# The latents' normalisation factors spread, and the latents scaled, ahead of the last projection panel

## The chip, the core and the metric

One core of a Trainium2 chip runs the whole program. The metric is the device time of one execution in microseconds (us); less is better. Five engines have instruction streams of their own: TensorE (PE, matmuls), VectorE (DVE), ScalarE (ACT), GpSimd (POOL) and SyncE (SP, which here only issues DMAs).

## What is computed

Two layers of a diffusion backbone over 512 latent tokens and 256 context tokens of width 1024. Layer 0 has 8 heads of multi-head latent attention (MLA) and 8 heads of neighbourhood attention side by side, then SwiGLU; layer 1 has sliding-window attention, then SwiGLU. What matters here is how the MLA heads get their inputs:

```
p = modulate(h) @ w_in                       # one input projection for all of layer 0
q_lat = rms_norm(p[..., :256], q_norm)       # query latent: 2 panels of 128 features
c_kv  = rms_norm(p[..., 256:384], kv_norm)   # key/value latent: 1 panel
k_rope = p[..., 384:416]
q = q_lat @ w_q_up ;  keys and values from c_kv
...
def rms_norm(x, gain):  return x * rsqrt(mean(x * x) + EPS) * gain
```

The neighbourhood heads take q, k, v from the other 1536 columns of the same projection.

## The kernel before

Features lie on the 128 partitions and the 768 tokens along a row (512 latents, `LATS`, then 256 context tokens, `CTXS`). A float32 product is made of three matmuls of operands split in a high and a low half (`split`: a cast on ACT, L340, and a difference on DVE, L341).

**Projections** (`projections`). One panel is 128 output features: `project` loads its weights, splits them and issues 24 matmuls of 512 columns for the latents (8 steps over the 16 high and low tiles of the modulated input, three each), then 24 of 256 columns for the context, each half in one PSUM bank, which ACT then evicts (L718). Banks come in a fixed rotation of tags by `PG` ("stsdtsd"); tag `d` has two buffers, `s` three, `t` two, `o` one. First come the panels of head pairs 0 and 1, then what the string `AFTER` says: 0, 1, 2 are the three latent panels (`lat_raw`), k the rope part, 5 to 8 the panels of q and k of pairs 2 and 3 (kept raw in `raws`), and r is `latent_roots`: squares of the three latents on ACT, sums over features on PE, square root on ACT, and the reciprocal on DVE (L973), which leaves one factor for each token in a column tile `sm`, six columns for each of two groups (the key/value latent, and the two query latents). Meanwhile DVE works on the modulation vectors (L234: products with an accumulated sum, two for each of two vectors), which `bg` deals out.

**Neighbourhood pairs** (`na_jobs`). For each of four head pairs, jobs make scores (L725, L726), take them into SBUF with bias and running minimum on DVE (L535, from `pss` banks; with `zeros` for context queries, with the bias tiles `nb` and `b` for the others), exponentials on ACT (L531, summing), transpose the result 128 x 128 on PE (L479), copy it (L470 on DVE, L471 on ACT) and multiply by the values (L525). `ORDER` says which other work is stepped beside which pair: `split_pair(2)` beside the first; `latent_norms` (n) and `split_pair(3)` beside the second; `mla_prepare` (m) beside the third. `split_pair` casts raw q on ACT (L1015), takes its low half on DVE (L1017), the same for k (L1023, L1024), and copies halves between partitions by DMAs on SP's queue. The bias tiles of the next pair come over that queue too.

**The step that is edited.** `latent_norms` runs `gained`. For each group, `gain` spreads the factors: a PE transposition of a column, broadcast to 128 x 128, for each block of 128 tokens (L346, four for the latents and two for the context, in a bank of tag `d` from `PQ`), which gives every partition the row of factors. DVE then scales each tile in place by gain and factor (L949), reading that bank. Then `gained` splits the scaled tiles.

**What sets the order.** The program is recorded as it is written; a scheduler then orders each engine's stream, by its own estimate of times and by priorities (work beside a pair has a lower one, `LOWER`), and each engine runs its stream in that order. Tiles of one tag share a ring of buffers: a tile waits until its buffer's last reader is done. The buffers of tag `b` that the pair splits and bias tiles take are those of the modulated input, which the last panel is the last to read.

Of the kernel before, what the change touches and what calls it, by code (L numbers as in the profile page):

```python
# [52 lines left out]
OUTQ = 1  # L53
E1, EF = 1, 1
ORDER = ("2", "n3", "m", "")
AFTER = "012k5r678"
PACE = (3, 3, 3, 3, 5, 5, 5, 6, 5, 5, 3, 2)
KC = (1, 1, 0)
VP = 0
# [39 lines left out]
def hybrid_kernel(ctx: ExitStack, tc, I, out):  # L99
# [6 lines left out]
    def T(tag, shape, dt=F32):  # L106
        count[0] += 1
        if tag not in SIZES:
            return sb.tile(shape, dt, tag=tag, name=f"{tag}_{count[0]}", bufs=BUFS.get(tag, 1))
        n = int(np.prod(shape[1:]))  # L110
        t = sb.tile([P, SIZES[tag] // (2 if dt == mybir.dt.bfloat16 else 4)], dt, tag=tag, name=f"{tag}_{count[0]}",
                    bufs=BUFS[tag])[: shape[0], :n]
        if len(shape) == 3:
            t = t.rearrange("p (a b) -> p a b", a=shape[1])
        return t

    def B(dt=F32, tag="b"):
        return T(tag, [P, NT], dt)
# [7 lines left out]
    def PG():  # L126

        ring[0] += 1
        return PS("stsdtsd"[ring[0] % 7])

    V, S, G, PE = nc.vector, nc.scalar, nc.gpsimd, nc.tensor
# [4 lines left out]
    def f(ap):  # L136
        return ap.bitcast(F32) if ap.dtype == F32R else ap
# [186 lines left out]
    def PQ():  # L324
        return PS("d")
# [10 lines left out]
    def split(src, eng=None, dst=None):  # L336

        p, n = src.shape
        h, lo = dst or (B(F32R), B(F32R))
        marks["cast"] = S.copy(h[:p, :n], src)  # L340
        marks["split"] = (eng or V).tensor_tensor(lo[:p, :n], src, f(h[:p, :n]), op=ALU.subtract)  # L341
        return h, lo

    def spread(o, col):

        return PE.transpose(o, col, ident)  # L346
# [337 lines left out]
    def put_q(ts, scale, hi=None, lo=None, after=()):  # L684


        def use(src, c):
            for side, t in enumerate(ts):
                r, x = slice(64 * side, 64 * side + 64), slice(64 - 64 * side, 128 - 64 * side)
                if scale is None:  # L690
                    behind((hi or S.copy)(t[r, c], src[r]), *after)
                    (lo or G.tensor_tensor)(t[x, c], src[r], f(t[r, c]), op=ALU.subtract)
                    continue
                S.activation(t[r, c], src[r], AF.Copy, scale=scale)
                V.scalar_tensor_tensor(t[x, c], src[r], scale, f(t[r, c]), op0=ALU.mult, op1=ALU.subtract)

        return use

    def put_k(ks, copies=True, hi=None):


        def use(src, c):
            for side, (k1, k2) in enumerate(ks):
                r, x = slice(64 * side, 64 * side + 64), slice(64 - 64 * side, 128 - 64 * side)
                (hi or S.copy)(k1[r, c], src[r])
                V.tensor_tensor(k2[r, c], src[r], f(k1[r, c]), op=ALU.subtract)
                if copies:
                    dma(k1[x, c], k1[r, c], G if dense[0] else None)
                    dma(k2[x, c], k2[r, c], G if dense[0] else None)
                else:  # L710
                    S.copy(k1[x, c], src[r])
                    V.tensor_tensor(k2[x, c], src[r], f(k1[r, c]), op=ALU.subtract)

        return use

    def put(t, rows=P, scale=1.0):
        def use(src, c):
            marks["put"] = S.activation(t[:rows, c], src, AF.Copy, scale=scale)  # L718

        return use  # L720
# [18 lines left out]
    def project(src, use, cols=(LATS, CTXS), m=P, every=2, eng=None, w=None, get=PQ):  # L739

        w = w or load_w(src, KT, m, eng)
        for c in cols:
            o, _ = banks([c], get, m)[0]
            for k in range(KT):
                mm3([(o, c)], (w[0][:, k : k + 1], w[1][:, k : k + 1]), A[k : k + 1], k == 0, k == KT - 1)
                if k % every == every - 1:
                    yield
            use(o, c)
# [26 lines left out]
    def first_norm(acc, c):  # L775
        n, d = (c.stop - c.start) // P, PM()
        col = T("sm", [P, 6, 2]).rearrange("p a b -> p (a b)")[:, :n]
        ins = [PE.matmul(d[:, i : i + 1], acc[:, i * P : (i + 1) * P], ones[:, :1], start=True, stop=True) for i in range(n)]
        run(ins[0], ins[-1])
        root = S.activation(col, d[:, :n], AF.Sqrt, bias=eps, scale=1.0 / D)  # L780
        V.reciprocal(col, col)
        return root, col
# [76 lines left out]
    _, diag = first_norm(acc, LATS)  # L859
# [8 lines left out]
    for c in range(4):  # L868
# [16 lines left out]
        if c == 3:  # L885
            _, diag = first_norm(acc, CTXS)
# [45 lines left out]
    def put_rope(t, tabs, swap, rows=P, scale=1.0, tag="b", eng=None):  # L932
        def use(src, c):
            if c is LATS:
                rope(t[:rows, c], src, tabs, swap, scale, tag, eng)
            else:
                S.activation(t[:rows, c], src, AF.Copy, scale=scale)

        return use

    def gain(tiles, g0, col):

        for c in (LATS, CTXS):
            d, n = PQ(), c.stop - c.start
            for i in range(n // P):
                at = c.start // P + i
                spread(d[:, i * P : (i + 1) * P], col[:, at : at + 1].to_broadcast([P, P]))
            for j, t in enumerate(tiles):
                V.scalar_tensor_tensor(t[:, c], t[:, c], gains[:, g0 + j : g0 + j + 1], d[:, :n], op0=ALU.mult, op1=ALU.mult)  # L949
        return tiles  # L950

    roots = []

    def latent_roots():

        d, m = PG(), NT // P
        groups = (lat_raw[2:], lat_raw[:2])
        col = T("sm", [P, 6, 2]).rearrange("p a b -> p (a b)")[:, : m * len(groups)]
        for i, tiles in enumerate(groups):
            acc = None  # L960
            for t in tiles:
                s = B(tag="p")
                S.activation(s, t, AF.Square)
                if acc is not None:
                    G.tensor_tensor(s, s, acc, op=ALU.add)
                acc = s
            for j in range(m):
                PE.matmul(d[:, i * m + j : i * m + j + 1], acc[:, j * P : (j + 1) * P], ones[:, :1], start=True, stop=True)
        for i, tiles in enumerate(groups):
            c = slice(i * m, i * m + m)  # L970
            S.activation(col[:, c], d[:, c], AF.Sqrt, bias=eps, scale=1.0 / (P * len(tiles)))
            roots.append(col[:, c])
        V.reciprocal(col, col)  # L973

    def gained(groups):

        for i, (tiles, g0) in enumerate(groups):
            res = [split(t, V) for t in gain(tiles, g0, roots[i])]
            groups[i] = res
            yield  # L980

# [3 lines left out]
    ON, lat_raw, kr = [], [None] * 3, []  # L985
# [3 lines left out]
    def projections():  # L989

        for p in range(2):
            yield from project(I["w_in0"][p], put_q(sets[p][0], 0.125), get=PG)
            yield from project(I["w_in0"][p + 4], put_k(sets[p][1], KC[0]), get=PG)
        for x in AFTER:
            if x in "012":
                lat_raw[int(x)] = B()
                yield from project(I["w_in0"][8 + int(x)], put(lat_raw[int(x)]), get=PG)
            elif x == "r":
                latent_roots()
            elif x == "k":  # L1000
                kr.append(B())
                yield from project(I["w_kr"], put_rope(kr[0], rope0, SWAP8, 32, tag="p"), m=32, get=PG)
            else:
                raws.append(B(tag="p"))
                i = int(x) - 5
                yield from project(I["w_in0"][(2, 6, 3, 7)[i]], put(raws[i], scale=(0.125, 1.0)[i % 2]), get=PG)
# [44 lines left out]
    def latent_norms():  # L1051
        groups = [(lat_raw[2:], 2), (lat_raw[:2], 0)]
        yield from gained(groups)
        wu["ckv"], wu["cq"] = groups
# [101 lines left out]
    for i, _ in enumerate(projections()):  # L1156
        n, r = PACE[i // 8], i % 8
        bg((r + 1) * n // 8 - r * n // 8)
# [45 lines left out]
    for k in range(KT):  # L1204
        t = B()
# [339 lines left out]
    for k in range(KT):  # L1545
        t = dr.tile([P, NL], F32, name=f"parked{k}")
# [78 lines left out]
    for k in range(KT):  # L1625
        t = B()
# [182 lines left out]
```

## Time and profile before

| | |
|---|---|
| median of 3 runs | 1558.43 us (1556.03 to 1559.27) |
| profiled execution | 1556.28 us, its span 1554.5 us |
| busy in the span | PE 97%, DVE 76%, ACT 49%, POOL 14% |
| granted TensorE clock | 0.996 |
| the six scalings L949 | 185.4 to 194.9 us |
| the reciprocal L973 | 156.3 us |

Busy time of PE goes by modelled ends, since matmuls are pipelined: a matmul's duration is longer than the distance to the next one's start. Times are counted from the start of the span. A row of the order of time has start, duration, engine, line, operation, written<-read and shape; in brackets stand the engine's idle time ahead of it and what ended it.

### The profile page before, as it was taken

How to read it: one execution, taken by the hardware profiler on the slowest of the kernel's cores; microseconds unless marked ns; L12 is line 12 of the kernel's file. 1: busy time of each engine (PE TensorE's matmuls, PEld its weight loads, DVE VectorE, ACT ScalarE, POOL GpSimd, SP SyncE). 2: the span in 40 equal slices, each digit the busy share in tenths (PEclk: the TensorE clock that was granted, in tenths of full speed). 3: DMA queues.
4: the chain of work that ended last, by engine and by line, in shares of the span. 5: the costliest groups of instructions: out<-in, count | busy, mean ns of one | idle time of the engine just before them, and what ended most of it. 6: DMA issues, size and time to landing. Idle time of an engine off the chain costs nothing.

```text
span 1554.5 us, 26373 instructions
## 1 busy us (share of the span) xinstructions
PE 1514.4 (97%) x9936; PEld 1364.3 (88%) x9936; DVE 1177.2 (76%) x2409; ACT 768.7 (49%) x1531; POOL 218.8 (14%) x272
## 2 busy tenths in 40 slices
PE   6999999999999999999999999999999999999998
PEld 4888887877999998999989998877889899899998
DVE  4799777686867686877768677779967779678685
ACT  4532587684555242433324335558746455454453
POOL 0021043110111102012021122650021000000001
PEclk9999999999999999999999999999999999999999
DMA  9674532023633636447365493200224223324222
GB/s 329 240 224 146 159 127 65 12 85 133 227 132 126 232 104 221 173 146 284 120 257 184 162 345 127 68 28 2 96 83 136 82 72 134 107 76 136 88 89 89
DMA packets 78736, 219.37 MB, mean 141 GB/s; under 512 B 10480, under 2 KB 17520, under 8 KB 78608
## 3 DMA queue, kind: packets, MB, share of 16 engines
q1 hardware_dynamic: 60848, 147.30, 28.4%
q0 software_dynamic: 16608, 68.81, 12.6%
q8 instruction: 78, 1.28, 0.3%
q10 hardware_dynamic: 1152, 1.57, 0.3%
q14 instruction: 50, 0.41, 0.1%
HBM read 186.97 MB, written 23.07 MB: 135 GB/s over the span
## 4 chain that ended last, share of the span: by engine, by line
PE 83%; DVE 8%; DMA 3%; ACT 3%; issue 2%; POOL 0%; SPq 0%; DVEq 0%; ACTq 0%; POOLq 0%
PE pss L1380 5%; PE pss L1379 5%; PE pss L1378 5%; PE pso L525 5%; PE psd L314 4%; PE pss L317 4%; PE pss L314 4%; PE psd L316 4%; PE pss L316 4%; PE psd L317 4%; PE pst L314 3%; PE pst L317 3%; PE pst L316 3%; PE pst L1380 3%; PE pst L1378 3%; PE pst L1379 3%
## 5 line engine op out<-in xcount | busy, mean ns | idle before, releaser
L303 ACT CAST wh<-wr 128x1024 fp32r<-128x1024 f32 (+2 forms) x148 | 115.5, 795 | 218.6 <-DMA wr<-in_w_dn_dram 44.2
L304 DVE TENSOR_TENSOR wl<-wr,wh 128x1024 fp32r<-128x1024 f32 (+2 forms) x145 | 130.7, 908 | 79.7 <-ACT wh L303 75.8
L531 ACT ACTIVATE p<-p,sm 128x512 f32<-128x512 f32 (+3 forms) x144 | 104.9, 730 | 28.4 <-DVE sm L535 28.0
L1378 PE MATMUL pss<-b,wh 128*128 128x384 f32 (+1 forms) x346 | 107.7, 312 | 0.6 <-ACT b L340 0.6
L1379 PE MATMUL pss<-b,wh 128*128 128x384 f32 (+1 forms) x346 | 107.9, 312 | 0.1
L1380 PE MATMUL pss<-b,wl 128*128 128x384 f32 (+1 forms) x346 | 107.2, 312 | 0.0
L270 DVE CUSTOM_DVE_ANT_0 p<-rope,cond 128x1024 bf16<-128x1024 f32 x64 | 76.8, 1219 | 15.4 <-DMA rope<-in_mod_w_dram 15.0
L316 PE MATMUL psd<-b,wh 128*128 128x512 f32 (+2 forms) x254 | 88.4, 348 | 0.1
L314 PE MATMUL psd<-b,wh 128*128 128x512 f32 (+2 forms) x214 | 78.7, 368 | 1.5 <-ACT b L444 0.6
L525 PE MATMUL pso<-ph,b 128*64 128x256 f32 (+1 forms) x384 | 78.1, 363 | 1.2 <-DVE ph L470 1.0
L525 PE MATMUL pso<-pl,b 128*64 128x256 f32 (+1 forms) x384 | 78.5, 363 | 0.0
L317 PE MATMUL psd<-b,wl 128*128 128x512 f32 (+2 forms) x214 | 77.0, 360 | 0.0
L260 POOL DMA_DIRECT2D rope<-in_mod_w_dram x48 | 25.6, 533 | 324.3 <-DVE mod L270 302.7
L1378 PE MATMUL pst<-b,wh 128*128 128x384 f32 (+1 forms) x226 | 70.6, 312 | 0.6 <-ACT p L1428 0.6
L1380 PE MATMUL pst<-b,wl 128*128 128x384 f32 (+1 forms) x226 | 70.6, 312 | 0.6 <-DVE wl L1366 0.6
L1365 ACT CAST wh<-pl 128x512 fp32r<-128x512 f32 x78 | 44.8, 619 | 52.2 <-PE pss L1379 22.8
L1379 PE MATMUL pst<-b,wh 128*128 128x384 f32 (+1 forms) x226 | 70.5, 312 | 0.0
L1365 ACT CAST wh<-wr 128x1024 fp32r<-128x1024 f32 x39 | 41.0, 1051 | 58.3 <-PE pst L1379 14.7
L316 PE MATMUL pss<-b,wh 128*128 128x256 f32 (+3 forms) x216 | 68.4, 317 | 0.0
L314 PE MATMUL pss<-st,wh 128*128 128x512 f32 (+2 forms) x198 | 67.1, 339 | 0.3 <-ACT wh L303 0.3
L317 PE MATMUL pss<-st,wl 128*128 128x512 f32 (+2 forms) x198 | 67.2, 339 | 0.1
L1378 PEld LDWEIGHTS pss<-b,wh 128*128 128x128 f32 x346 | 65.6, 190 | 1.1 <-ACT b L340 0.9
(603 smaller groups left out, 5275.3 us busy)
## 6 DMA issues: line engine op xcount, KB each, us to landing
wr<-in_w_gu_dram SPq DMA_DIRECT2D x88, 512.0 KB, 4.0
rope<-in_mod_w_dram POOLq DMA_DIRECT2D x48, 512.0 KB, 3.9
wr<-in_w_dn_dram SPq DMA_DIRECT2D x73, 256.0 KB, 2.9
wr<-in_w_out_dram SPq DMA_DIRECT2D x32, 512.0 KB, 4.3
p<-home POOLq DMA_DIRECT2D x40, 384.0 KB, 5.6
home<-p POOLq DMA_DIRECT2D x40, 384.0 KB, 5.3
wr<-in_w_in_dram SPq DMA_DIRECT2D x21, 512.0 KB, 4.2
ph<-in_mod_w_dram SPq DMA_DIRECT2D x24, 256.0 KB, 3.1
```

What stands on the lines that cost most here:

```text
L270: behind(V.tensor_tensor_reduce(out=T("p", [P, D], mybir.dt.bfloat16), in0=w, in1=cond[:, v, :], op0=ALU.mult, op1=ALU.add, scale=1.0, sca ...
L303: behind(S.copy(h, r), *after[:1])
L304: behind((G if eng else V).tensor_tensor(lo, r, f(h), op=ALU.subtract), *after[1:])
L314: ins = PE.matmul(o, wh[:, k], mh[:, c], start=first and k == 0, stop=False)
L316: PE.matmul(o, wh[:, k], ml[:, c], start=False, stop=False)
L317: PE.matmul(o, wl[:, k], mh[:, c], start=False, stop=last and k == n - 1)
L525: ins = PE.matmul(o[64 * i : 64 * i + 64, c], v(kt), t, start=n == 0, stop=n == len(moving[i]) - 1)
L531: S.activation(p[:, c], p[:, c], AF.Exp, bias=nm, scale=-1.0, accum_out=dn)
L1365: S.copy(h, t)
L1378: PE.matmul(o, wh, xh, start=first and k == 0, stop=False, skip_group_check=not first)
L1379: PE.matmul(o, wh, xl, start=False, stop=False, skip_group_check=not first)
L1380: PE.matmul(o, wl, xh, start=False, stop=k == 3, skip_group_check=not first)
```

## The change

`AFTER` gets a "g" between panel 7 and panel 8: there `gain` is called for both groups, so that the factors are spread and the latents scaled in the projections. `gained` keeps only the splits, which stay beside the second pair.

```diff
-AFTER = "012k5r678"
+AFTER = "012k5r67g8"
...
     def gained(groups):
 
-        for i, (tiles, g0) in enumerate(groups):
-            res = [split(t, V) for t in gain(tiles, g0, roots[i])]
+        for i, (tiles, _) in enumerate(groups):
+            res = [split(t, V) for t in tiles]
             groups[i] = res
             yield
...
             elif x == "r":
                 latent_roots()
+            elif x == "g":
+                for i, (tiles, g0) in enumerate(((lat_raw[2:], 2), (lat_raw[:2], 0))):
+                    gain(tiles, g0, roots[i])
```

Three lines are added ahead of L1003, so L1015, L1017, L1023 and L1024 of before are L1018, L1020, L1026 and L1027 of the change.

Where the instructions stand. PE at the end of the projections: before, the last matmul of the last panel (its context half, `pst`, behind its latents' half, `psd`) and then the first pair's scores.

```order
L316 MATMUL pst_1735<-b_113,wh_1696 128x256
L317 MATMUL pst_1735<-b_112,wl_1697 128x256
L725 MATMUL pss_1783<-st_654,st_652 128x256
L726 MATMUL pss_1783<-st_655,st_652 128x256
L725 MATMUL pss_1793<-st_656,st_653 128x256
L726 MATMUL pss_1793<-st_657,st_653 128x256
L725 MATMUL pss_1816<-st_654,st_652 128x256
L726 MATMUL pss_1816<-st_655,st_652 128x256
```

In the change the first group's six spreads stand ahead of that panel's context half; behind that half come (with the rest of the latents' half after the last row):

```order
L317 MATMUL pst_1757<-b_112,wl_1719 128x256
L725 MATMUL pss_1805<-st_654,st_652 128x256
L726 MATMUL pss_1805<-st_655,st_652 128x256
L725 MATMUL pss_1815<-st_656,st_653 128x256
L726 MATMUL pss_1815<-st_657,st_653 128x256
L725 MATMUL pss_1838<-st_654,st_652 128x256
L346 MATMUL psd_1703<-ident_r_86,sm_1504 128x128 x4
L346 MATMUL psd_1710<-ident_r_86,sm_1504 128x128 x2
L726 MATMUL pss_1838<-st_655,st_652 128x256
L725 MATMUL pss_1838<-st_654,st_652 128x256
L726 MATMUL pss_1838<-st_655,st_652 128x256
L314 MATMUL psd_1722<-b_98,wh_1718 128x512
```

The two halves of the panel have changed places, five of the scores come ahead of the second group's spreads, and the latents' half, whose bank is the one that `psd_1703` had, comes last.

ACT at the same place, before:

```order
L718 ACTIVATE p_1693<-psd_1700 128x512
L718 ACTIVATE p_1693<-pst_1735 128x256
L1015 CAST b_1803<-p_1415 128x768
L531 ACT_TABLE_LOAD
L531 ACTIVATE p_1784,sm_1773<-p_1784,sm_1774 128x256
```

and in the change:

```order
L718 ACTIVATE p_1715<-pst_1757 128x256
L1018 CAST b_1825<-p_1415 128x768
L1026 CAST b_1827<-p_1527 128x768
L718 ACTIVATE p_1715<-psd_1722 128x512
L531 ACT_TABLE_LOAD
```

The two casts of pair 2's split have moved ahead of the eviction of the latents' half; the table load and the first exponentials stand behind it.

DVE at the same place, before: the last products of the modulation (each followed by its sum, `128x1`) and the first takes.

```order
L234 ISA p_1729,mod_323_1409<-ph_1725,cond_66 128x512
L234 ISA mod_323_1409 128x1
L234 ISA p_1731,mod_323_1409<-pl_1727,cond_66,mod_323_1409 128x512
L234 ISA mod_323_1409 128x1
L238 SCALAR_TENSOR_TENSOR mod_323_1409<-mod_323_1409,modb_89 128x8
L234 ISA p_1760,mod_331_1435<-ph_1725,cond_66 128x512
L234 ISA mod_331_1435 128x1
L234 ISA p_1762,mod_331_1435<-pl_1727,cond_66,mod_331_1435 128x512
L234 ISA mod_331_1435 128x1
L238 SCALAR_TENSOR_TENSOR mod_331_1435<-mod_331_1435,modb_89 128x8
L535 ISA p_1784,sm_1774<-pss_1783,zeros_95 128x256
```

In the change, from the first scaling on:

```order
L949 SCALAR_TENSOR_TENSOR b_1220<-b_1220,mla_gain_690,psd_1693 128x512
L949 SCALAR_TENSOR_TENSOR b_1220<-b_1220,mla_gain_690,psd_1699 128x256
L234 ISA p_1753,mod_323_1409<-pl_1749,cond_66,mod_323_1409 128x512
L234 ISA mod_323_1409 128x1
L238 SCALAR_TENSOR_TENSOR mod_323_1409<-mod_323_1409,modb_89 128x8
L949 SCALAR_TENSOR_TENSOR b_1038<-b_1038,mla_gain_690,psd_1703 128x512
L949 SCALAR_TENSOR_TENSOR b_1132<-b_1132,mla_gain_690,psd_1703 128x512
L949 SCALAR_TENSOR_TENSOR b_1038<-b_1038,mla_gain_690,psd_1710 128x256
L949 SCALAR_TENSOR_TENSOR b_1132<-b_1132,mla_gain_690,psd_1710 128x256
L1020 TENSOR_TENSOR p_1415<-p_1415,b_1825 128x768
L234 ISA p_1782,mod_331_1435<-ph_1747,cond_66 128x512
L234 ISA mod_331_1435 128x1
```

The scalings stand among the last products, and the low halves of pair 2's split ahead of the last two products and thus of the first takes.

DVE in the second pair, from the first take with its bias tile, before:

```order
L535 ISA p_2065,sm_1950<-pss_2060,nb_1951 128x512
L535 ISA sm_1950 128x1
L535 ISA p_1960,sm_1950<-pss_1959,zeros_95 128x256
L535 ISA sm_1950 128x1
L1024 TENSOR_TENSOR st_2055<-p_1693,st_2054 128x768
L949 SCALAR_TENSOR_TENSOR b_1220<-b_1220,mla_gain_690,psd_2007 128x512
L470 COPY pl_1974<-pst_1969 128x512
L455 RECIPROCAL sm_2126<-sm_1773 128x12
L470 COPY pl_1998<-pst_1993 128x512
L535 ISA p_1984,sm_1950<-pss_1983,zeros_95 128x256
L535 ISA sm_1950 128x1
L535 ISA p_2089,sm_1950<-pss_2082,nb_1951 128x512
```

and in the change:

```order
L535 ISA p_2065,sm_1972<-pss_2060,nb_1973 128x512
L535 ISA sm_1972 128x1
L341 TENSOR_TENSOR b_2030<-b_1220,b_2029 128x768
L455 RECIPROCAL sm_2126<-sm_1795 128x12
L341 TENSOR_TENSOR b_2045<-b_1038,b_2044 128x768
L470 COPY pl_2020<-pst_2015 128x512
L341 TENSOR_TENSOR b_2049<-b_1132,b_2048 128x768
L535 ISA p_1982,sm_1972<-pss_1981,zeros_95 128x256
L535 ISA sm_1972 128x1
L535 ISA p_2006,sm_1972<-pss_2005,zeros_95 128x256
L535 ISA sm_1972 128x1
L470 COPY ph_2027<-pst_2022 128x512
```

The scaling is gone, and the three low halves of the latents (L341) stand behind that take in one run, ahead of the second takes with `zeros`.

## The prediction

> **What bounds the kernel now.** I read the page first, then busy time by stretches of time, then the chain of waits, then DVE, PE, ACT and the DMA queue in order of time around the place that is edited. The page gives the span; the profiled execution took 1556.28 us, 2.15 below the median of 1558.43, so the sum below is a difference, made on the profiled execution and then set on the median.
>
> ```profile
> span 1554.5 us, 26373 instructions
> PE 1514.4 (97%) x9936; PEld 1364.3 (88%) x9936; DVE 1177.2 (76%) x2409; ACT 768.7 (49%) x1531; POOL 218.8 (14%) x272
> ```
>
> PE is busy 97% by its modelled ends: hardly any change can win more than the few waits that PE has left. By stretches (columns: span, then busy time of each engine with its instructions, granted clock, DMA share, GB/s):
>
> ```profile
> 140.00:160.00 20.00, 20.00 (x126) 18.04 (x125) 19.43 (x51) 7.17 (x12) 2.30 (x1) 1.00 0.35 106
> 160.00:168.00 8.00, 8.00 (x48) 7.09 (x47) 3.31 (x12) 0.75 (x2) 0.00 (x0) 1.00 0.08 17
> 168.00:180.00 12.00, 11.43 (x85) 9.42 (x84) 10.95 (x32) 11.86 (x29) 0.00 (x0) 1.00 0.74 193
> 180.00:190.00 10.00, 9.39 (x80) 7.89 (x79) 7.71 (x22) 6.86 (x22) 0.00 (x0) 1.00 0.96 276
> 190.00:200.00 10.00, 9.82 (x79) 7.40 (x77) 9.45 (x26) 7.28 (x18) 0.00 (x0) 1.00 0.89 258
> 200.00:210.00 10.00, 9.68 (x81) 8.19 (x81) 10.00 (x24) 10.00 (x27) 2.39 (x1) 1.00 0.77 255
> ```
>
> Up to 168 us (the projections) PE has no idle time while DVE is full until 160 and then half empty. From 168 to 210, the first two neighbourhood pairs, DVE or ACT is full in three stretches of four and PE idles 0.57 + 0.61 + 0.18 + 0.32 = 1.68 us. The clock is granted in full throughout. The chain of waits there:
>
> ```profile
> 168.50 0.73 ACT b L1015
> 169.25 5.06 DMA b<-b
> 174.84 4.64 DMA b<-b
> 180.06 3.36 DMA nb<-in_nb_dram
> 183.58 0.25 DVE p L535
> 186.81 0.66 PE pst L479 x4
> ```
>
> It runs through the split of pair 2: cast, its copies on SP's queue, then the bias tile of the second pair queued behind them, and only then DVE and PE.
>
> **The change part by part.** The six scalings (L949) with their twelve transposing matmuls (L346) leave the second pair. Nothing is added. In the stretch of 180 to 200 us the scalings take on DVE (columns: span, DVE busy, clock, DMA):
>
> ```profile
> 180.00:200.00 20.00, 3.47 (x6) 1.00 0.92 267
> ```
>
> Where they go on DVE, and what stands around there now:
>
> ```profile
> 160.16 0.69 DVE L234 CUSTOM_DVE_ANT_0 p<-ph,cond 128x512 bf16<-128x512 f32 x1
> 160.89 0.75 DVE L234 CUSTOM_DVE_ANT_0 p<-pl,cond,mod 128x512 bf16<-128x512 f32 x1
> 168.35 0.42 DVE L535 CUSTOM_DVE_ANT_0 p<-pss,zeros 128x256 f32<-128x256 f32 x1 [4.90 <-PE pss L726]
> 170.38 0.95 DVE L1017 TENSOR_TENSOR p<-p,b 128x768 fp32r<-128x768 f32 x1
> 183.58 0.69 DVE L535 CUSTOM_DVE_ANT_0 p<-pss,nb 128x512 f32<-128x512 f32 x1 [2.29 <-DMA nb<-in_nb_dram]
> 185.41 0.74 DVE L949 SCALAR_TENSOR_TENSOR b<-b,mla_gain,psd 128x512 f32<-128x512 f32 x1
> ```
>
> DVE waits 4.90 us for the first scores: room for 3.47, if the scalings can run in it. What they wait for, and what waits for them, is on PE:
>
> ```profile
> 159.57 0.40 PE L314 MATMUL psd<-b,wh 128*128 128x512 f32 x1
> 165.04 0.28 PE L314 MATMUL pst<-b,wh 128*128 128x256 f32 x1
> 167.91 0.28 PE L725 MATMUL pss<-st,st 128*128 128x256 f32 x1
> 168.03 0.28 PE L726 MATMUL pss<-st,st 128*128 128x256 f32 x1
> 171.19 0.33 PE L479 MATMUL pst<-ident_r,p 128*128 128x128 f32 x1 [0.41 <-ACT p L531]
> 180.47 0.60 PE L346 MATMUL psd<-ident_r,sm 128*128 128x128 f32 x4
> 180.91 0.60 PE L479 MATMUL pst<-ident_r,p 128*128 128x128 f32 x4
> 186.21 0.43 PE L346 MATMUL psd<-ident_r,sm 128*128 128x128 f32 x2 [0.44 <-DVE b L949]
> 186.81 0.33 PE L479 MATMUL pst<-ident_r,p 128*128 128x128 f32 x1 [0.17 <-DVE pl L470]
> ```
>
> Paces from these rows: the latents' half of the last panel takes 165.04 - 159.57 = 5.47 us for 24 matmuls (0.23 each), its context half 167.91 - 165.04 = 2.87 (0.12 each), a spread (180.91 - 180.47) / 4 = 0.11. DVE started 0.32 us after the second score was issued (168.03, 168.35): I use 0.3 for PE to DVE, and 0.2 back.
>
> *Loss 1, PE at the last panel.* Six spreads end at 159.57 + 0.66 = 160.2. The order then has the context half first (to 163.1), five score matmuls (163.7), the other six spreads (164.4) and three scores (164.7). The latents' half, which writes the PSUM buffer that the second group's factors hold, waits until DVE has read them twice. DVE's product of 160.16 and the first two scalings are over before; the third starts at 163.7 + 0.33 + 0.3 = 164.35, and two of 0.7 end at 165.75. PE goes on at 165.9: a wait of 1.2 us that was not there, and the panel ends at 171.4.
>
> *Loss 2, the first exponentials.* On ACT they stand behind the eviction of that half, and behind the table load:
>
> ```profile
> 165.24 0.60 ACT L718 ACTIVATE p<-psd 128x512 f32<-128x512 f32 x1 [5.08 <-PE psd L317]
> 168.39 0.83 ACT L1015 CAST b<-p 128x768 fp32r<-128x768 f32 x1
> 169.24 1.28 ACT L531 ACT_TABLE_LOAD   x1
> 170.53 0.51 ACT L531 ACTIVATE p<-p,sm 128x256 f32<-128x256 f32 x1
> ```
>
> Eviction 171.6 to 172.2, load to 173.5; the first transposition followed the first exponential's start by 171.19 - 170.53 = 0.66, so it comes at 174.15. Before it stood at 171.19, with the second near score (0.6 us of matmuls) ahead of it; now that comes behind, to 174.85 against 171.3. Of these 3.55 us, 12 x 0.11 = 1.3 is the spreads' own work, which is paid back later. PE has lost 2.2 us by then, Loss 1 included. Its bounds: 1.2 if ACT finds room for the load earlier, 3.5 if the spreads' time does not come back.
>
> A page speaks of that load. The Trainium skill, "ScalarE: Activation LUTs", section "What ACT_TABLE_LOAD costs", states about 1283 ns and another 1380 ns of drain for each switch. The load's row agrees with the first (1.28); no row has the second, since the cast ends at 169.22, the load starts at 169.24 and the exponential at 170.53. By the page the sum would be 1.4 us higher; I go by the rows.
>
> *DVE and SP behind it.* DVE's low half of pair 2's split now stands ahead of the last two products and of the first scores. It waits for ACT's cast, whose buffer is free after the sixth matmul of the latents' half: 165.9 + 6 x 0.23 + 0.3 = 167.6, cast to 168.4. Then 0.95 + 0.69 + 0.95 + 0.75: the first scores are taken at 171.7, 3.3 us later than 168.35, but with 3.47 + 2 x 0.95 = 5.4 us of work done. DVE is 2.1 ahead in work, waits some 1.2 for the second near score, and no longer needs the 2.29 for the bias tile: SP issues it behind the fewer copies, once the first pair's bias tile has been read for the last time (about 176), landing 3.4 later, at 179.5, before DVE asks. About 3 us of lead by 197 us.
>
> *Gain.* What PE makes of that lead is bounded below by its waits that name the moved work or stand right behind it, 0.44 + 0.17 = 0.6, and above by all of DVE's freed time, 3.47. PE's own idle time from 171.3 to 210 is 1.68 - 0.41 = 1.3, but PE also paces its short matmuls by DVE there without counting as idle. I take 2.2, the middle of 1.3 and DVE's lead of 3.1: neither row is nearer.
>
> *Costing nothing:* the latents' low halves (L341) stay on DVE and are only closer together; POOL has two instructions exchanged; DMAs are the same in number and size, and the queue of weight loads on SP is unchanged up to the first pair. Cover for all of them is PE's 97%; without it each L341 would cost its 0.95.
>
> Sum: 2.2 - 2.2 = 0.0, so 1556.3 for the profiled execution and 1558.4 for the median. The bounds give 1.2 - 3.5 = -2.3 and 3.5 - 0.6 = +2.9, that is 1556.1 to 1561.3, all within 0.2% (3.1 us), which is about what a measurement of this kernel tells from no change (the three runs spread by 3.2).
>
> **The rivals.** *Faster: the chain of copies decides.* What ended last there was cast, copies, bias tile. If DVE and PE simply follow that chain, the take of 183.58 moves to 179.5 and the rest with it: -4.0 us, 1554.4. For it: the chain's unbroken 15 us and DVE's 2.29 of waiting. Against: DVE is full before (10.95 of 12) and reaches that take only after about 8 us of work that starts later.
>
> *Slower: the latents' splits in front of the second takes.* In the new order three low halves stand on DVE in one run ahead of the second pair's second zero-bias takes, and PE's next scores need the banks that these takes free. Before, the scalings were spread between takes. The run costs 3 x 0.95 = 2.85; with the loss of 2.2, and only 0.6 recovered, +4.4 us, 1562.8. It decides once PE has nothing else to issue in that time, that is when more than 0.9 of the 2.85 falls on PE on top of an unrecovered 2.2. For it: PE's row at 186.21 waits for DVE in just such a place. Against: PE still has the first pair's weighted sums to issue there.
>
> *Nothing happens:* PE at 97% is the bound, its matmuls are the same, and both loss and gain vanish in its queue; 1558.4 too, on the forecast's side.
>
> **How the numbers follow.** Forecast, with the case that nothing happens: 0.51. Faster rival 0.26, slower rival 0.23; each lies past the 3.1 us, so these are also the chances by sign. Behind the second pair the order differs in many small places, up to the end of the latent heads and again in the first feed-forward layer, which I cannot price; it is why the two rivals keep half. The range goes from a little below the faster rival, 1553.6, to the slower one, 1562.8; the likeliest case alone has 1556.1 to 1561.3.
>
> **What would show it.** Loss 1: PE idle by about 1.2 us near 165, waiting for DVE L949, ahead of the panel's 512-wide matmuls. Loss 2: the first transposition at about 174. DVE's first take near 171.7, with a wait for ACT's cast ahead of L1020. The bias tile issued near 176 and no wait of DVE for it. By 210 us the two kernels level again within 2 us. It would be wrong if PE never waits at the panel (then faster), or if PE waits over 1 us for DVE around 185 to 190 (then slower).

## The result and the profile after

The changed kernel takes 1566.43 us (median of 6 runs, 1563.82 to 1567.67); the kernel before takes 1559.24 beside it (median of 6, 1556.03 to 1563.54). The ratio is 1.0040, 95% interval 1.0024 to 1.0057: 6.2 us slower by the ratio (7.2 by the medians), where 1558.4 was forecast, and above the range's upper end of 1562.8. The profiled execution took 1566.97 us. Its page, span and busy time:

```profile
span 1565.2 us, 26391 instructions
PE 1518.4 (97%) x9936; PEld 1368.8 (87%) x9936; DVE 1178.3 (75%) x2409; ACT 769.3 (49%) x1531; POOL 218.9 (14%) x272
```

The engines did the same work as before (DVE 1178.3 against 1177.2 us). The same stretches of time as in the prediction, of the changed kernel:

```profile
160.00:168.00 8.00, 6.98 (x53) 6.52 (x52) 5.44 (x13) 0.78 (x3) 0.00 (x0) 1.00 0.00 0
168.00:180.00 12.00, 10.25 (x55) 8.95 (x54) 7.88 (x24) 8.59 (x20) 0.00 (x0) 0.86 0.72 186
180.00:190.00 10.00, 8.94 (x73) 6.85 (x72) 8.93 (x23) 8.88 (x21) 0.00 (x0) 1.00 0.86 244
190.00:200.00 10.00, 9.27 (x82) 7.88 (x82) 8.57 (x24) 8.18 (x24) 0.00 (x0) 1.00 0.86 223
200.00:210.00 10.00, 8.47 (x69) 7.38 (x67) 7.51 (x22) 7.37 (x21) 2.37 (x1) 1.00 0.75 232
```

PE idles 1.02 us up to 168 and 5.07 from 168 to 210 (12 + 10 + 10 + 10, less the busy times), against nothing and 1.68 before, and the granted clock falls to 0.86 between 168 and 180 (it is near 0.5 for 3.5 us of them, called the half clock below). DVE is no longer full from 168 to 180 (7.88 of 12, before 10.95). PE's larger waits that are new or longer than in the kernel before, in order of time:

```profile
166.32 0.47 PE L314 MATMUL psd<-b,wh 128*128 128x512 f32 x1 [1.02 <-DVE b L949]
174.65 0.33 PE L479 MATMUL pst<-ident_r,p 128*128 128x128 f32 x1 [1.44 <-ACT p L531]
185.21 0.63 PE L479 MATMUL pst<-ident_r,p 128*128 128x128 f32 x4 [0.35 <-DVE ph L470]
187.28 0.40 PE L525 MATMUL pso<-ph,b 128*64 128x256 f32 x1 [0.71 <-DVE ph L470]
192.71 0.38 PE L725 MATMUL pss<-st,st 128*128 128x256 f32 x1 [0.73 <-DVE sm L535]
205.69 0.33 PE L479 MATMUL psd<-ident_r,p 128*128 128x128 f32 x1 [1.53 <-ACT p L531]
334.66 0.50 PE L1122 MATMUL pss<-st,st 96*128 96x512 f32 x1 [1.47 <-DVE sm L535]
```

The first two are the prediction's two losses. The next four stand where a gain was forecast. The last is in the latent heads, 170 us later. DVE around the edited place:

```profile
164.77 2.19 DVE L949 SCALAR_TENSOR_TENSOR b<-b,mla_gain,psd 128x512 f32<-128x512 f32 x4 [1.45 <-PE psd L346]
168.85 0.96 DVE L1020 TENSOR_TENSOR p<-p,b 128x768 fp32r<-128x768 f32 x1 [1.89 <-ACT b L1018]
171.88 0.42 DVE L535 CUSTOM_DVE_ANT_0 p<-pss,zeros 128x256 f32<-128x256 f32 x1
181.07 0.69 DVE L535 CUSTOM_DVE_ANT_0 p<-pss,b 128x512 f32<-128x512 f32 x1 [1.23 <-DMA b<-p]
188.34 0.68 DVE L535 CUSTOM_DVE_ANT_0 p<-pss,nb 128x512 f32<-128x512 f32 x1
188.95 0.95 DVE L341 TENSOR_TENSOR b<-b,b 128x768 fp32r<-128x768 f32 x1
```

The second pair's first take of a bias tile (`nb`), 183.58 before, is now at 188.34, with no wait for the tile but 4.8 us later. SP's queue there:

```profile
180.61 0.58 SPq L134 DMA_DIRECT2D nb<-in_nb_dram  x1
196.04 1.61 SPq L134 DMA_DIRECT2D nb<-in_nb_dram  x2
197.74 0.38 SPq L134 DMA_DIRECT2D wr<-in_w_ukv_dram  x1
```

The second pair's tile is issued at 180.61, where 176 was forecast and 180.06 stood before. Behind the third pair's tiles stands the load of `w_ukv`, the latents' up-projection weights.

A word on comparing positions: profiles of one program differ by up to 2 us at 140 us, ahead of anything edited. Where one kernel is said to stand so much behind another "at 440 us", it is the median difference in start of the same ACT and DVE instructions near there, less that at 140 us. By 440 us, behind the latent heads, the first profile after stands 7.2 us behind the first before.

### The profile page after: what moved, and what is told of

It is laid out like the page before. It is cut to its first block, busy times and chain, and to the rows that moved or that the text cites. A ratio compares the mean times of both kernels' runs of the same rounds, so it can differ in the third digit from the quotient of the medians.

```text
span 1565.2 us, 26391 instructions
## 1 busy us (share of the span) xinstructions
PE 1518.4 (97%) x9936; PEld 1368.8 (87%) x9936; DVE 1178.3 (75%) x2409; ACT 769.3 (49%) x1531; POOL 218.9 (14%) x272
## 4 chain that ended last, share of the span: by engine, by line
PE 82%; DVE 9%; ACT 3%; issue 3%; DMA 2%; POOL 1%; DVEq 0%; SPq 0%; ACTq 0%; POOLq 0%
PE pss L1383 5%; PE pss L1381 5%; PE pss L1382 5%; PE pso L525 4%; PE pss L317 4%; PE pss L314 4%; PE psd L314 4%; PE pss L316 4%; PE psd L316 4%; PE psd L317 4%; PE pst L314 3%; PE pst L317 3%; PE pst L316 3%; PE pst L1383 3%; PE pst L1381 3%; PE pst L1382 3%
```

## The experiments

Three theories at the start. *Theory 1*: the two losses stand as forecast, and a third comes from them that was not, half a clock behind the stretch in which PE was starved. *Theory 2*: the new order of takes and splits on DVE costs PE its waits from 185 on. *Theory 3*, formed on the first traces: the load of `w_ukv` comes late and holds ACT. Theory 4 is on the latent heads.

### The changed kernel again, and with the idle time filled

**again**: no edit.

> The changed kernel once more, unaltered, for a second profile. Theory 1 (sparse PE, then half clock): the loss begins at the last panel. PE waits about 1.0 us for the factors' PSUM buffer near 166, is busy only some 1.25 of 3 us between 172 and 175 (eviction, table load, first exponential), and the granted clock is 0.50 from about 175 to 178.5; all of that must come again, since the program is the same. The lower clock near 335 and near 787 follows stretches that are no sparser than ones of the kernel before that kept the clock, so it may come or not. Theory 2 (order): the loss is the waits of PE for DVE and ACT between 185 and 206 (0.35, 0.71, 0.73, 1.53 us), and the clock near 175 is chance: then it is absent here about as often as not, with the same time. Either way 1563 to 1568 us.

**fill**: five matmuls whose result nobody reads; `seen` holds the score matmuls in the order written, `runs` the last matmul of each step of a panel.

```diff
+        if turns[0] == 1:
+            at, x, k = seen[5]
+            for i in range(5):
+                fill.append(behind(PE.matmul(outs[1], x, k[:, :512], start=True, stop=True), *(fill[-1:] or [at, *runs[-16:]])))
         for i, b in enumerate(blocks):
-            ins = PE.transpose(o[:, i * P : (i + 1) * P], b, ident)
+            ins = behind(PE.transpose(o[:, i * P : (i + 1) * P], b, ident), *fill[-1:])
```

> The changed kernel with five 512-wide matmuls of no use put on PE behind the last panel's latents' half, ahead of the next near scores; the order is otherwise the same on every engine. They take 5 x 0.23 = 1.1 us of a stretch in which PE idled 1.75. Theory 1: PE is busy some 2.4 of the 3 us from 172 to 175, the granted clock stays at 1.00 from 175 to 178.5, and the kernels' later work stands about 1.8 us earlier than in the changed kernel by 180: 1563 to 1566, 1.5 to 2 less than the repeated changed kernel in the same call if nothing later changes. Theory 2: clock and time as in the changed kernel, or 0.5 us worse since the near scores come 0.6 to 1.1 us later. Should the clock fall all the same, the sparse PE is not its cause.

Measured: again 1565.58 us, 1.0041 (1.0026 to 1.0055); fill 1566.48, 1.0050 (1.0036 to 1.0063). Again has the waits of 1.02 and 1.42 us, the half clock behind them, and 2.06 us of waiting for ACT at 206; its clock also halves behind that wait, and not near 335 as in the first profile after. Two stretches of time (columns as above) of the first profile after:

```profile
172.00:175.00 3.00, 1.25 (x8) 0.94 (x8) 2.03 (x11) 2.88 (x7) 0.00 (x0) 1.00 1.02 259
175.00:178.50 3.50, 3.50 (x19) 3.50 (x19) 1.40 (x4) 3.10 (x10) 0.00 (x0) 0.51 0.63 149
```

and of fill, whose work stands 0.8 us later on its own clock:

```profile
173.00:176.00 3.00, 2.00 (x15) 1.64 (x13) 1.90 (x11) 2.97 (x7) 0.00 (x0) 1.00 1.02 281
176.00:179.50 3.50, 3.50 (x33) 3.50 (x33) 2.57 (x7) 3.50 (x12) 0.00 (x0) 1.00 0.88 202
```

With PE busy 2.00 of 3 us and not 1.25, the clock stays at 1.00, so starving PE does make the half clock there, as theory 1 said. It is no rule for other places: in half_qG, a run of a later section, PE is busy for less of 3 us and keeps the clock.

```profile
194.25:197.25 3.00, 1.06 (x7) 0.83 (x7) 2.76 (x5) 1.07 (x3) 0.00 (x0) 1.00 0.44 118
197.25:200.75 3.50, 3.17 (x22) 2.20 (x23) 3.50 (x10) 2.58 (x7) 0.00 (x0) 1.00 0.93 240
```

And the time does not fall. The profile of fill, its fastest run, stands 2.0 us ahead of the first after at 182 us, and only 4.2 us behind the first of before at 440 (after 7.2, again 6.8), having none of the other half clocks either; the medians do not follow it. Theory 1's price, 1.5 to 2 us, is not confirmed for the whole run; fill_qG takes it up again.

### The bank, and a third of the step

**bank_o**: the factors go to the bank of the weighted sums.

```diff
-    def gain(tiles, g0, col):
+    def gain(tiles, g0, col, get=PQ):
...
-            d, n = PQ(), c.stop - c.start
+            d, n = get(), c.stop - c.start
...
-                    gain(tiles, g0, roots[i])
+                    gain(tiles, g0, roots[i], lambda: PS("o"))
```

> The changed kernel with the factors in the PSUM bank of the weighted sums (pso) in place of the panels' bank (psd), so that the last panel's latents' half does not wait for the scalings; in its order that half stands ahead of the context half again, as before the change. Theory 1: no wait of PE near 166, the eviction near 166 again, the first transposition near 172.5 (1.3 us of spreads behind 171.2), no half clock near 175; about 3 us better than the changed kernel by 180, and 1559 to 1563 in the end. Theory 2: the scalings and the split of pair 2 still stand among the first takes on DVE, so the waits between 185 and 206 stay, and the time is 1564 to 1567.

**half**: only the key/value latent at the new place.

```diff
-                for i, (tiles, g0) in enumerate(((lat_raw[2:], 2), (lat_raw[:2], 0))):
+                for i, (tiles, g0) in enumerate(((lat_raw[2:], 2),)):
...
-        for i, (tiles, _) in enumerate(groups):
-            res = [split(t, V) for t in tiles]
+        for i, (tiles, g0) in enumerate(groups):
+            res = [split(t, V) for t in (gain(tiles, g0, roots[i]) if i else tiles)]
```

> Only the key/value latent is scaled at the new place (2 of the 6 scalings, 6 of the 12 transposing matmuls); the two query latents are scaled ahead of their split in the second pair, as before the change. The last panel's halves stand in the changed order, latents' half last, but nothing waits for the scalings. Theory 1: no wait near 165, the latents' half ends near 169.6, evicted at 170.2, the table loaded at 171.5, first transposition near 172.2: 1 us later than before the change and 2.4 earlier than with it. PE still idles 1 to 2 us there, so the clock may or may not fall; 1560 to 1564. Theory 2: as much of the order as was moved for the split of pair 2 is still moved, but two scalings stand between the second takes again: 1563 to 1567.

Measured: bank_o 1564.51, 1.0033 (1.0022 to 1.0044); half 1564.36, 1.0036 (1.0022 to 1.0050). In neither does PE wait at the panel, and in neither does the clock fall near 175; yet most of the loss stays: both are above theory 1's ranges and in theory 2's. The rows that take its place, ACT and PE in half, then in bank_o:

```profile
203.39 1.04 ACT L303 CAST wh<-wr 128x1024 fp32r<-128x1024 f32 x1 [4.39 <-DMA wr<-in_w_ukv_dram]
205.20 0.33 PE L479 MATMUL psd<-ident_r,p 128*128 128x128 f32 x1 [4.03 <-ACT p L531]
```

```profile
203.95 1.04 ACT L303 CAST wh<-wr 128x1024 fp32r<-128x1024 f32 x1 [2.81 <-DMA wr<-in_w_ukv_dram]
206.51 0.50 PE L314 MATMUL psd<-b,wh 128*128 128x512 f32 x1 [2.12 <-ACT pl L471]
```

ACT stops at a cast whose weights have not landed; behind it stand exponentials and evictions for which PE waits nearly as long. That is theory 3.

### The load on another queue

One edit to four kernels: `w_ukv` is loaded by POOL's queue and not SP's. In bank_o nothing else moves on any engine.

```diff
-    def load_w(src, kt, m, eng=None, tag=None, after=()):
+    def load_w(src, kt, m, eng=None, tag=None, after=(), queue=None):
...
-        dma(r, src)
+        dma(r, src, queue)
...
-        wu["kv"] = load_w(I["w_ukv"], 2, 512, G)
+        wu["kv"] = load_w(I["w_ukv"], 2, 512, G, queue=G)
```

> bank_o with one DMA moved from SP's queue to POOL's: the load of the latents' up-projection weights (w_ukv, 512 KB). The order on PE, DVE and ACT is bank_o's row for row. Theory 3: in the changed kernels SP issues this load late, behind the bias tiles (nb) that wait for the second pair's last takes, and it lands 6.5 us after its issue in place of 4.5; ACT stops at the cast of it (L303, 2.8 us in bank_o, 1.11 before the change) with the exponentials behind it, PE waits 2.12 for ACT at 206.5, and the clock halves after that. By it the load is issued near 190, ACT's wait for it is below 0.7, PE's wait near 206 is below 0.6, the clock stays at 1.00 between 200 and 215, and the time falls by 2 to 3.5 from bank_o's 1564.5, to 1561 to 1562.5. Theory 2 (it is the order of the takes on DVE): the exponentials come no sooner, another wait takes the place, 1564 to 1565.

> half with the same load on POOL's queue (behind 210 us the order differs in a few places). In half ACT waited 4.4 us for it and PE 4.03 us at 205, with the clock halved; next to this half lost only 1.2 us against the kernel before by 195. Theory 3: both waits fall below 1 us, no half clock near 205, 1559.5 to 1561: that is, within 0.1% of the kernel before. Theory 2: 1563 to 1565, as half (1564.4).

> The changed kernel with the same load on POOL's queue (some reordering behind 203 us). Theory 3: the wait near 166 (1.02), the first transposition near 174.7 and the half clock from 175 to 178.5 stay; ACT's wait for the load (2.6 and 3.2 us in its two profiles) falls below 0.7 and PE's near 205 (1.53, 2.06) below 0.6. Time 1562.5 to 1564.5, 1.5 to 3.5 below the changed kernel. Theory 2: 1565 to 1567.

> The kernel before the change with the same load on POOL's queue, to see what this does without the change: ACT waited 1.11 us for it there and PE 0.32 us at 205. Theory 3: 1558.5 to 1559.6, no more than 0.6 below the kernel before, so that what the move brings to the changed kernels is a repair of what the change did. If it is faster by 2 us or more, the load was a general weakness and not the change's loss.

Measured, against the kernel before: bank_o_qG 1558.28 us, 0.9993 (0.9983 to 1.0003); half_qG 1556.15, 0.9976 (0.9967 to 0.9985); after_qG 1561.60, 1.0010 (1.0002 to 1.0019); before_qG 1554.90, 0.9969 (0.9957 to 0.9982). ACT's wait for the load is gone in all four. All gain more than expected, and the one that was to gain at most 0.6 us gains 4.3. By its own words that expectation failed: the load is a weakness of the kernel before too. after_qG against before_qG is 1.0010 - 0.9969 = 0.0041, or 6.4 us, the same as with the load on SP. Against before_qG, bank_o_qG has 0.0024 left (0.0033 with the load on SP) and half_qG 0.0007 (0.0036). So theory 3 explains most of why half was no better and part of it for bank_o, and not why the changed kernel is slower.

**before_again**: no edit.

> The kernel before the change, for a second profile. Its first profile (1556.28) was one of its fastest runs: 30 later ones have a median of 1559.2. Moving the load of w_ukv made it 4.3 us faster in the medians, but only 1.9 by 440 us in the profiles. If the load is what makes its runs differ, a typical run has ACT waiting more than 1.11 us at L303, PE more than 0.32 near 205, and perhaps a half clock behind it; if not, these rows repeat and the difference lies elsewhere.

Measured: 1560.05 us in this one run. Less its start, it repeats the first profile within 0.1 us up to the eviction at 194 us; then (ACT and PE):

```profile
202.22 1.05 ACT L303 CAST wh<-wr 128x1024 fp32r<-128x1024 f32 x1 [2.82 <-DMA wr<-in_w_ukv_dram]
206.00 0.50 PE L314 MATMUL psd<-b,wh 128*128 128x512 f32 x1 [1.52 <-ACT pl L471]
```

and it stays 1.7 us behind to 440. ACT's 1.11 us of the first profile was a good draw, as expected if the load makes the runs differ. PE's 0.32 there is another wait, for a copy on DVE, and is back with 0.30; what is new is the 1.52 for ACT. The rest of before_qG's gain is not explained: at its second pair's first take with a bias tile, ahead of the load, it already stands 2.0 us ahead of both profiles of before.

With the load out of the way the loss can be read. PE's waits over 0.15 us from 160 to 340 us in before_qG:

```profile
172.70 0.33 PE L479 MATMUL pst<-ident_r,p 128*128 128x128 f32 x1 [0.41 <-ACT p L531]
204.53 0.35 PE L725 MATMUL pss<-b,b 128*128 128x192 f32 x1 [0.71 <-DVE sm L535]
224.08 0.47 PE L314 MATMUL psd<-b,wh 128*128 128x512 f32 x1 [0.50 <-DVE b L470]
239.34 0.66 PE L479 MATMUL pst<-ident_r,p 128*128 128x128 f32 x4 [0.63 <-DVE b L462]
319.68 0.50 PE L1119 MATMUL pss<-st,st 128*128 128x512 f32 x1 [1.15 <-DVE sm L535]
```

and in after_qG:

```profile
166.38 0.47 PE L314 MATMUL psd<-b,wh 128*128 128x512 f32 x1 [1.02 <-DVE b L949]
172.42 0.39 PE L725 MATMUL pss<-st,st 128*128 128x256 f32 x1 [0.34 <-DVE sm L535]
174.69 0.33 PE L479 MATMUL pst<-ident_r,p 128*128 128x128 f32 x1 [1.42 <-ACT p L531]
186.35 0.40 PE L525 MATMUL pso<-ph,b 128*64 128x256 f32 x1 [0.44 <-DVE ph L470]
191.78 0.38 PE L725 MATMUL pss<-st,st 128*128 128x256 f32 x1 [0.74 <-DVE sm L535]
241.30 0.66 PE L479 MATMUL pst<-ident_r,p 128*128 128x128 f32 x4 [0.63 <-DVE b L462]
243.29 0.50 PE L725 MATMUL pss<-st,st 128*128 128x512 f32 x1 [0.17 <-DVE sm L535]
322.10 0.50 PE L1122 MATMUL pss<-st,st 128*128 128x512 f32 x1 [1.09 <-DVE sm L535]
332.24 0.50 PE L1122 MATMUL pss<-st,st 96*128 96x512 f32 x1 [1.48 <-DVE sm L535]
```

Up to the first transposition: 1.02 + 0.34 + 1.42 = 2.78 against 0.41, a loss of 2.37. From there to 260: 0.44 + 0.74 + 0.63 + 0.17 = 1.98 against 0.71 + 0.50 + 0.63 = 1.84, no gain. In the latent heads: 2.57 against 1.15, a loss of 1.42. Together 3.9 us of idle time, of 5.1 by which after_qG stands behind at 440. By position, 3.0 of the 5.1 stand there at 250 us and 2.0 come between 250 and 340, where the clock is granted in full; so the half clock can hold some 0.5, and the other 0.6 that the waits do not show lies in the latent heads. From 440 to the end another 1.3 us come. Their cause is open, and they need not be the change's: the two profiles of the untouched kernel move apart by 1.3 us there too.

The same sums come near for the other two: bank_o_qG idles 1.6 us more than before_qG up to 260 and 1.4 more in the latent heads (3.7 us behind at 440, 2.0 of them from 250 on), half_qG 2.1 and none (1.6 behind, none from 250 on). And by the ratios of these runs, all on one chip and each good to about 1.5 us: bank_o_qG, without the wait and with the panel's halves in the old order, has 2.65 of the 6.4 us less; half_qG, with two scalings moved in place of six, another 2.65; 1.1 stay.

### The two terms left, and another place

**fill_qG**: fill's edit on after_qG, nothing else in the order moved.

> after_qG with the five idle-filling matmuls of fill; the order is otherwise after_qG's on every engine. By the profiles after_qG stands 5.1 us behind before_qG at 440 us and 6.4 at the end; some 1.9 of it should be the half clock from 175 to 178.5. Theory 1: no half clock there, 1.3 to 1.9 us less at 440 us, 1559.5 to 1560.5 in the end. Rival (what is gained is paid back, as half of the lead of fill over the changed kernel seemed to be by 250): no gain left at 440 us, 1561 to 1562.

**fill_qG_v7**: one product more on DVE.

```diff
-            (V if "l" in EV and p < 1 else G).tensor_tensor(lo[r], x[r], f(hi[r]), op=ALU.subtract)
+            (V if h == 7 and x is kn[p] else G).tensor_tensor(lo[r], x[r], f(hi[r]), op=ALU.subtract)
```

> fill_qG with one of POOL's products moved to DVE: the low half of the eighth latent head's keys (L1113, 64x768). In all six profiles with the changed order of the latent heads POOL starts this product 0.3 to 0.4 us ahead of DVE's L1174, which then takes 1.74 us in place of 0.41, and PE waits 1.47 us for the take behind it; in the four profiles with the old order L1174 takes 0.41 and PE does not wait. Theory 4 (DVE held by POOL): L1174 takes 0.41, PE's wait of 1.47 falls below 0.3, and the kernel is 1.2 to 1.5 us faster than fill_qG by 440 us (1558 to 1559.5), less what the product itself costs DVE (0.95 by an L341, behind the take). Rival (DVE is late there in any case, the long L1174 only shows it): PE waits as long for another row, no gain.

**g_last_qG**: on after_qG, the step one place later.

```diff
-AFTER = "012k5r67g8"
+AFTER = "012k5r678g"
```

> Factors and scalings placed behind the last panel, not ahead of it, with the load on POOL's queue. The panel's halves stand in the order of before, and its eviction and the table load are not delayed; the second group's three scalings stand between the first and the second zero-bias takes on DVE, and 12 spreads (1.3 us) among the first scores on PE. Theory 1 (panel order, wait and clock make the loss, scaling early is harmless): no wait of PE at the panel, first transposition near 172.5, no half clock, 1556 to 1558. Theory 2 (each instruction put ahead of the first takes delays the neighbourhood heads): the takes of the second near scores come 3 us later and PE waits for them, 1559 to 1562.

Measured: fill_qG 1561.34, 1.0020 (1.0007 to 1.0034); fill_qG_v7 1561.70, 1.0025 (1.0014 to 1.0035); g_last_qG 1561.27, 1.0024 (1.0013 to 1.0036).

fill_qG has no half clock near 175, and stands 0.4 us further behind at 440 than after_qG: the rival held. Its PE is 1.6 us ahead of after_qG at the score of 178.40, then waits 0.84 us for DVE at 181 and 0.57 and 0.71 at 185 and 187, where after_qG waits 0.44 in all. DVE idles 2.54 us ahead of the take that PE waits for; the profile names a transposition that had long ended, so it is likelier a copy on SP's queue. What the full clock wins is lost there in this profile; in fill's it was kept. So what the half clock costs is not settled, and no median shows a gain from filling.

fill_qG_v7. The rows of DVE and POOL in the latent heads of after_qG, then DVE and PE of fill_qG_v7 (whose lines stand 6 further down: L1180 is L1174, L1119 is L1113, L485 is L479):

```profile
329.50 1.75 DVE L1174 TENSOR_TENSOR b<-b,b 128x256 fp32r<-128x256 f32 x1
...
329.13 1.82 POOL L1113 TENSOR_TENSOR st<-b,st 64x768 fp32r<-64x768 f32 x1 [7.72 <-ACT st L1112]
```

```profile
329.73 0.41 DVE L1180 TENSOR_TENSOR b<-b,b 128x256 fp32r<-128x256 f32 x1
331.12 0.96 DVE L1119 TENSOR_TENSOR st<-b,st 64x768 fp32r<-64x768 f32 x1
...
332.97 0.33 PE L485 MATMUL psd<-ident_r,p 128*128 128x128 f32 x1 [0.75 <-ACT p L537]
355.41 0.33 PE L485 MATMUL pst<-ident_r,wr 128*128 128x128 f32 x1 [1.76 <-DVE ph L471]
```

Without POOL's product beside it L1174 takes 0.41 us, and PE's wait of 1.48 is gone: theory 4 is shown for the wait, and not for its price. A wait of 0.75 us for ACT stands in its place. At 340 us the kernel stands 1.1 us better than fill_qG, but 1.0 of that was there at 250, since it lacks that profile's waits at 181 and 185. At 355 PE waits 1.76 us for an eviction on DVE (0.58 in after_qG), and by 400 the kernel stands 1.2 us behind fill_qG; the product's 0.96 on DVE and small changes of the order behind it are what differs. No gain in the end.

g_last_qG has the old order of the halves and no wait at the panel, and its first transposition is 0.7 us later than before_qG's; then PE waits 0.48 and 0.82 us for DVE at 176 and 177, and the clock falls, near 178 and again near 335. It stands 2.6 us behind before_qG at 250 (after_qG 3.0) and 6.2 at 440. Theory 2 held here: it is not only the panel; six scalings among the first takes cost nearly as much when they stand behind the panel.

before_qG, the old order with the load on POOL's queue, is the fastest of all that were run.

## Why the prediction was wrong, step by step

*Loss 1*: right. PE waits 1.02 us at the panel for L949 (1.2 forecast; the 0.2 from DVE back to PE, for which the forecast had no row, measured 0.13, from the second scaling's end at 166.19 to 166.32).

*Loss 2*: right. On ACT, eviction, load and exponential come at 172.09, 172.70 and 174.00,

```profile
172.09 0.60 ACT L718 ACTIVATE p<-psd 128x512 f32<-128x512 f32 x1 [2.51 <-PE psd L317]
172.70 1.28 ACT L531 ACT_TABLE_LOAD   x1
174.00 0.51 ACT L531 ACTIVATE p<-p,sm 128x256 f32<-128x256 f32 x1
```

the first transposition at 174.65 (174.15 forecast; the profile started 0.4 late), and there is no drain beside the load, as the rows of before had it. The loss of 2.2 us is 2.37 by the waits in after_qG and before_qG.

*DVE and SP behind it*: DVE half right, SP wrong. The first take is at 171.88 behind a wait for ACT's cast, as forecast (171.7). But the bias tile was not issued near 176: ahead of it on SP's queue stand the split's copies, SP waits 4.9 us for earlier copies to land (4.2 before), and the tile left at 180.61, hardly later than before (180.06; 0.4 of the rest is the late start). The forecast had priced that issue by the last read of the first pair's tile. And DVE's work ahead of the first takes was not turned into a lead of 3 us: DVE then waited 2.16, 0.37 and 0.58 us for PE's scores, late themselves, and 1.23 for a copy (181.07), and the second pair's first `nb` take came 4.8 us later than before.

*Gain*: this is the step that failed. 2.2 us were taken, the middle between the waits that named the moved work (0.6) and DVE's lead. PE's waits from the first transposition to 260 us are 1.98 and 1.84 us with the load moved: the gain was nil. With the load on SP the 0.44 and 0.17 near 186 went, and 0.35, 0.71 and 0.73 took their place; in before_qG the 0.44 and 0.17 are gone without the change. By position, too, nothing was regained: level at 210 within 2 us was forecast, and at 250 the changed kernel stands 3.0 us behind, in the first pair of profiles and in the pair with the load moved. The middle rested on DVE's lead, and the lead did not come.

*Costing nothing*: the sentence on the unpriced order "up to the end of the latent heads" named a real cost and set none. after_qG and bank_o_qG fall back by 2.0 us there, half_qG by nothing. Some 1.4 of it is the wait at 334.66, which stands in every profile with all six scalings moved and POOL's product in place, and in none of the old order. That the collision of DVE with POOL makes this wait is shown; that the time comes back without it is not.

*Clock*: taken as full, it was not. Filling the gap brought no gain in the medians; what the half clock costs stays open.

*The slower rival* had the sign. Its place is there: the three L341 stand from 188.95 on, and PE waits 0.73 us at 192.71 for the take behind them, less than its 2.85. That PE would have nothing else to issue, which it took as decisive, was not tested alone. *The faster rival* fails with the SP step: the chain of copies did not get shorter. The sign that the prediction gave for being wrong, over 1 us of PE waiting for DVE around 185 to 190, is there in the first profile (0.35 + 0.71), and not in again (0.45).

So, for the pair with the load moved: 2.4 lost, where 2.2 was forecast; 2.2 to be regained, of which nothing came (0.1 more waiting); 0.5 more up to 250, which the half clock may hold; 2.0 in the latent heads, not priced, of which 1.4 are a wait that the traces show; and 1.3 behind 440, open. That is 6.4 us.

## What to carry to other kernels

Idle time of an engine is room only if what ends it does not come later for the work put in: here DVE's 4.90 us of waiting lay ahead of the first exponentials, and filling it put work in front of a chain through PE, ACT, DVE and SP, which then started 2.4 us later. Price a gain by the waits that name the moved work, and take the middle to an engine's freed time only where a view shows that it is that engine that PE follows. And read each in-order queue for what stands behind a waiting instruction: moving one weight load out from behind bias tiles brought the untouched kernel 4.3 us, not all of it explained.

## What was not expected of the hardware

A product of two SBUF operands on DVE took 1.75 us in place of 0.41 when POOL's product had started 0.37 us ahead of it; both ended within 0.3 us. The Trainium skill, "SBUF — State Buffer", section "SBUF: two separate sides", has the rule: DVE and GpSimd share a pair of ports under an exclusive lock, also for DVE operations with two SBUF inputs against a GpSimd operation that reads SBUF. The trace agrees, and moving POOL's product brought the 0.41 back.

The clock fell to half for about 3.5 us after a stretch of 3 us in which PE was busy 1.25, no single gap being over 1.5 us, in three profiles of three, and at the same place not after one with 2.00, in three of three. The busy share alone does not decide it: half_qG kept the clock after 1.06 of 3 us, and fill near 203 after 0.87. The Trainium skill, "TensorE: Matmul & The Clock Gate", section "HAM oscillation — how this bites in real kernels", warns of idle gaps over about 3.4 us; at this place much shorter ones were enough.
